# First modulation on TensorE with the condition stationary in four column groups, and the first norm's squares summed by TensorE

## The chip, the cores and the metric

One core of one Trainium2 chip runs the program; the other cores are idle. The metric is the time of one execution on the device, in microseconds, and the figure compared is the median of several executions.

The engines are named as in the profile: PE is TensorE (matmul), PEld its weight loads, DVE is VectorE, ACT is ScalarE, POOL is GpSimd, and SP is the queue that issues the DMAs here. Each engine takes its instructions in the order in which they stand in its own list and waits for semaphores; nothing overtakes within a list.

## The reference, cut to what matters

A block of a diffusion model with two layers. 512 latent tokens and 256 context tokens, 768 in all, have 1024 features. In each layer a condition vector, one for the latents and one for the context, is turned into six modulation vectors of 1024 values; the first two are the shift and the scale of the norm ahead of the input projection.

```
for i in range(DEPTH):                                    # DEPTH = 2
    mod_l = split(silu(c)     @ mod_w[i] + mod_b[i], 6)   # mod_w[i]: 1024 x 6144
    mod_c = split(silu(c_ctx) @ mod_w[i] + mod_b[i], 6)
    h_l = rms_norm(x,  g) * (1 + mod_l[1]) + mod_l[0]     # rms over the 1024 features
    h_c = rms_norm(xc, g) * (1 + mod_c[1]) + mod_c[0]
    p = h @ w_in[i]      # four mixers: rwkv7, differential attention, gla, grouped-query attention
    ...                  # mixers, w_out, second norm and modulation, convolutional feed-forward
```

All arithmetic that the kernel must match is float32. Nothing at all can be projected in layer 0 before the first two modulation vectors (16 blocks of 128 features, for two conditions) and the first norm's root are there.

## The kernel before

Activations lie with features on the 128 partitions: eight tiles of 128 features by 768 tokens, called x[0] to x[7]. A normed tile h[k] is kept as two numbers, a rounded high part and the rest, and so is each weight: ACT casts a staged weight (L377), POOL subtracts to get the rest (L378), and a product is three matmuls, high by high, high by rest and rest by high (`mm_feat`, L387; `mm_tok`, L710).

The part at issue is the head of the program, from the first instruction to the first matmul of the projection `glav` (L710) at 95.9 us. It is the generator `start()` in `run`, with `mod_first`, `squares` and `norm`:

- `mod_first` loads the condition twice. `cT` (128 x 16) is the condition with features on partitions. `silu_c` spreads each of the two condition vectors over all partitions (two tiles of 128 x 1024, each 512 KB of DMA) and applies silu to them with ACT (L432) and DVE (L433, L434).
- The eight x tiles are loaded (L1805); ACT squares each (L522), DVE adds the squares up over k (L526, six additions), and PE sums the two tiles that are left over the partitions (L552, 12 matmuls with one moving column). DVE takes the root by shifts and Newton steps (L400 to L407), spreads it along a diagonal (L563), and PE copies it to all partitions (L566); ACT brings it to SBUF (L570).
- Then a loop over k = 0 to 7. Pass k first makes the scale block and the shift block of its 128 features (`part(k)`), each by one of three ways, as the letters in `MOD0` say. P: PE, eight matmuls with a 128 x 128 weight block stationary and the two conditions moving (L465). D: DVE, one multiply with running sum per condition (L470, 128 x 1024). G: POOL multiplies (L474) and ACT sums (L475). Weights come in 16 loads of 512 KB (L461) into ten buffers. Then DVE scales x[k] into one shared tile y (L581), ACT writes the high part of h[k] (L583), and the rest comes from DVE (L585), or for k = 1, 4 and 7 from ACT and POOL (L588, L590). There is one y for all passes: the next pass's L581 waits until the last reader of y is done.
- PE meanwhile runs two projections that need h, `glaq` and `glak` (L387), 12 matmuls for each k as h[k] appears. When h[7] is done the mixers start; their first matmuls are those of `glav` (L710), six blocks of 128 tokens, each 24 matmuls over all eight k.

A scheduler takes the program in the order in which the code makes it, with `weave` mixing the generators of the mixers by due times, and decides in which order each engine gets its instructions. So an edit in the head can also move instructions of later parts.

## Time and profile before

| | us |
|---|---|
| three runs: median | 2406.66 |
| lowest, highest | 2404.67, 2407.81 |
| profiled execution, its time | 2409.76 |
| profiled execution, span from first to last instruction | 2408.0 |

| engine | busy us of the span | share | instructions |
|---|---|---|---|
| PE | 2209.1 | 92% | 15292 |
| DVE | 1457.9 | 61% | 3144 |
| POOL | 1040.0 | 43% | 1001 |
| ACT | 938.8 | 39% | 1756 |

The profiled execution is 3.1 us over the median. In the page's 40 slices PE is busy nine tenths almost everywhere; the first slice (60 us) has four tenths. The granted clock over the span is 0.945 of 2.4 GHz. In the column of the granted clock 1.00 stands also before the first record of a change, which is at 72.5 us here; ahead of that the clock is to be read from the length of the matmuls.

### The profile page before, as it was taken

The numbers are of one execution on the slowest core, as the hardware profiler recorded it, in microseconds if no ns is written. First come the engines' busy times: TensorE is split into PE (matmuls) and PEld (weight loads), VectorE is DVE, ScalarE is ACT, GpSimd is POOL, SyncE is SP. The second block draws the span as 40 slices with busy tenths as digits, with TensorE's granted clock in tenths as the row PEclk, the third lists the DMA queues.
The fourth block names the chain that finished last, engine by engine and source line by source line (L and its number), as shares of the span: only waits on it lengthen the run. The fifth ranks groups of instructions, "written<-read, shape, count | busy, mean of one in ns | idle before, by whom it ended". The sixth has DMA issues, their size and how long they took to land.

```text
span 2408.0 us, 40175 instructions
## 1 busy us (share of the span) xinstructions
PE 2209.1 (92%) x15292; PEld 1880.6 (78%) x15292; DVE 1457.9 (61%) x3144; ACT 938.8 (39%) x1756; POOL 1040.0 (43%) x1001
## 2 busy tenths in 40 slices
PE   4889988789988999999999989998899889999999
PEld 3777877577867888888888878777778668888888
DVE  6855689877774388655544662469777865322323
ACT  3333131355556242323222343322266474433333
POOL 3453465322331244434343645356433313655556
PEclk9889988688989999999999999998899899999999
DMA  6422264433225243333433432135433142233334
GB/s 246 146 90 73 78 186 123 106 87 84 65 65 167 66 136 118 114 105 108 137 100 111 152 102 62 58 92 153 116 86 94 47 123 84 89 104 89 104 92 136
DMA packets 232145, 258.48 MB, mean 107 GB/s; under 512 B 90960, under 2 KB 174224, under 8 KB 231952
## 3 DMA queue, kind: packets, MB, share of 16 engines
q1 hardware_dynamic: 231952, 255.92, 35.5%
q8 instruction: 120, 1.97, 0.3%
q14 instruction: 73, 0.60, 0.1%
HBM read 209.69 MB, written 37.77 MB: 103 GB/s over the span
## 4 chain that ended last, share of the span: by engine, by line
PE 63%; DVE 6%; POOL 4%; ACT 3%; issue 3%; DMA 2%; SPq 0%; POOLq 0%; DVEq 0%; ACTq 0%
PE pst L387 44%; PE pst L1552 5%; PE pst L427 4%; PE pst L710 3%; PE pst L977 2%; PE pst L1670 1%; PE pst L1675 1%; PE pst L941 1%; DVE mx L947 1%; ACT slab L949 1%; PE pst L944 1%; POOL slab L378 1%; DMA of<-slab 1%; POOL slab L846 0%; PE pst L1207 0%
## 5 line engine op out<-in xcount | busy, mean ns | idle before, releaser
L387 PE MATMUL pst<-slab,slab 128*128 128x512 f32 (+1 forms) x6552 | 1244.1, 351 | 20.5 <-ACT slab L583 7.4
L387 PEld LDWEIGHTS pst<-slab,slab 128*128 128x128 f32 x6552 | 1056.2, 191 | 201.5 <-ACT slab L583 10.8
L378 POOL TENSOR_TENSOR slab<-slab,slab 128x512 fp32r<-128x512 f32 (+1 forms) x428 | 576.8, 1357 | 724.1 <-ACT slab L377 701.9
L377 ACT CAST slab<-slab 128x512 fp32r<-128x512 f32 (+1 forms) x428 | 259.2, 614 | 575.4 <-PE pst L387 414.1
L710 PE MATMUL pst<-slab,slab 128*128 128x256 f32 (+1 forms) x1872 | 260.4, 300 | 11.0 <-POOL slab L378 11.0
L710 PEld LDWEIGHTS pst<-slab,slab 128*128 128x128 f32 x1872 | 249.1, 204 | 20.1 <-POOL slab L378 12.4
L623 DVE SCALAR_TENSOR_TENSOR slab<-pst,pp,slab 128x511 f32<-128x511 f32 x66 | 41.6, 658 | 305.1 <-ACT slab L620 305.1
L427 PE MATMUL pst<-cst,slab 128*128 128x128 f32 (+1 forms) x968 | 168.5, 309 | 51.2 <-POOL slab L1155 13.3
L497 DVE SCALAR_TENSOR_TENSOR slab<-slab,slab 128x512 bf16<-128x512 f32 x208 | 194.6, 936 | 6.1 <-DMA slab<-in_modw_dram 2.9
L427 PEld LDWEIGHTS pst<-cst,slab 128*128 128x128 f32 (+1 forms) x968 | 123.0, 155 | 79.5 <-POOL slab L1155 14.6
L1552 PE MATMUL pst<-slab,slab 128*128 128x128 f32 (+4 forms) x1328 | 167.3, 291 | 12.8 <-DVE slab L1606 4.0
L1552 PEld LDWEIGHTS pst<-slab,slab 128*128 128x128 f32 (+3 forms) x1328 | 139.6, 186 | 35.3 <-issue 10.5
L654 DVE SCALAR_TENSOR_TENSOR slab<-pst,fgate,slab 128x512 f32<-128x512 f32 (+1 forms) x144 | 88.0, 628 | 103.2 <-PE pst L387 103.1
L947 DVE TENSOR_REDUCE mx<-pst 128x1 f32<-128x768 f32 (+1 forms) x120 | 99.8, 846 | 33.5 <-PE pst L941 19.5
L949 ACT ACTIVATE slab<-pst,mx 128x768 f32<-128x768 f32 (+1 forms) x120 | 97.8, 816 | 46.5 <-DVE mx L947 43.0
L635 POOL TENSOR_TENSOR slab<-slab,slab 128x768 fp32r<-128x768 f32 (+1 forms) x44 | 74.0, 1683 | 63.9 <-ACT slab L634 63.9
L960 ACT ACTIVATE slab<-slab,r 128x768 f32<-128x768 f32 (+1 forms) x80 | 67.5, 852 | 9.3 <-DVE r L959 9.0
L977 PE MATMUL pst<-slab,slab 128*64 128x128 f32 x832 | 64.5, 287 | 2.8 <-DVE slab L424 1.5
L634 ACT CAST slab<-slab 128x768 fp32r<-128x768 f32 (+1 forms) x44 | 32.2, 732 | 84.1 <-DVE slab L631 84.0
L1639 POOL TENSOR_TENSOR slab<-cst,pcu 64x256 f32<-64x256 f32 x48 | 32.3, 673 | 72.7 <-PE pst L1552 18.5
L1425 DVE TENSOR_TENSOR slab<-slab,slab 96x31 f32<-96x31 f32 (+15 forms) x124 | 57.0, 459 | 8.7 <-DMA slab<-scrin 7.1
L629 ACT ACTIVATE slab<-slab 128x768 f32<-128x768 f32 (+1 forms) x44 | 32.5, 739 | 73.4 <-DVE slab L625 73.4
(309 smaller groups left out, 2707.7 us busy)
## 6 DMA issues: line engine op xcount, KB each, us to landing
slab<-in_wup_dram SPq DMA_DIRECT2D x88, 512.0 KB, 3.6
slab<-in_modw_dram SPq DMA_DIRECT2D x160, 256.0 KB, 3.0
slab<-in_wdn_dram SPq DMA_DIRECT2D x48, 512.0 KB, 3.5
slab<-in_win_dram SPq DMA_DIRECT2D x46, 512.0 KB, 3.7
slab<-in_modw_dram SPq DMA_DIRECT2D x16, 512.0 KB, 7.3
slab<-in_wout_dram SPq DMA_DIRECT2D x16, 512.0 KB, 3.5
slab<-in_xT_dram SPq DMA_DIRECT2D x16, 384.0 KB, 5.9
kb<-slab SPq DMA_DIRECT2D x8, 768.0 KB, 4.3
```

Of the source, the lines that this page charges most:

```text
L377: nc.scalar.copy(out=w[0], in_=st[:, k:k + q])
L378: nc.gpsimd.tensor_tensor(out=w[1], in0=st[:, k:k + q], in1=w[0].bitcast(F32), op=ALU.subtract)
L387: self.nc.tensor.matmul(ps[:, a:b], w[i][k][:, cols], x[j][k][:, a:b], start=(k == 0 and q == 0), stop=(k == nk - 1 and q == 2))
L427: self.nc.tensor.transpose(out, a.bitcast(F32) if a.dtype != F32 else a, self.c["ident"])
L497: self.tc.keep_in_program_order(nc.vector.scalar_tensor_tensor(out=junk, in0=w, scalar=1.0, in1=self.sc[s][:, e * hd:(e + 1) * hd], op0=AL ...
L635: nc.gpsimd.tensor_tensor(out=HL[:, 1, :n], in0=th[:, :n], in1=HL[:, 0, :n].bitcast(F32), op=ALU.subtract)
L654: nc.vector.scalar_tensor_tensor(out=x[m][:, a:b], in0=ps[:, a:b], scalar=gate[:, m, s:s + 1], in1=x[m][:, a:b], op0=ALU.mult, op1=ALU.add)
L710: self.nc.tensor.matmul(ps[:, :n], h[i][k][:, t * P:(t + 1) * P], w[j][k], start=(k == 0 and q == 0), stop=(k == KD - 1 and q == 2))
L947: nc.vector.tensor_reduce(out=mx, in_=sv, axis=AX.XY, op=ALU.max, negate=True)
L949: nc.scalar.activation(out=p[m][:, a:].rearrange("p (e c) -> p e c", e=2 - a // hb), in_=sv, func=AF.Exp, bias=mx, accum_out=lsum[:, m:m + 1])
L977: nc.tensor.matmul(acc[64 * e:64 * e + 64, :P], vs[e][:, i + j], aT[:, 256 * j + P * e:256 * j + P * e + P], start=(first and j == 0), sto ...
L1552: mm = lambda o, a, b, pos: nc.tensor.matmul(o, a, b, start=True, stop=True, tile_position=pos)
```

## The change

- Layout on the host: the 16 weight blocks of the first two modulation vectors are packed as eight pairs. Pair i holds blocks i (shift) and 8 + i (scale), 1024 input features by 256 output columns. Each pair is loaded in two halves of 512 KB into a ring of three pairs.
- `mod_open`: silu is applied to `cT` alone, and the two conditions are written into a zeroed tile c32 of 128 x 8 x 32, so that for each of the eight feature groups there is a stationary matrix of 32 columns, two of them not zero.
- `mod_pair`: for each pair eight matmuls, c32 stationary (32 columns), the weights moving (256 columns, float32). Feature group k goes to column group k mod 4 of the array, so that four partial sums stand on partitions 0, 32, 64 and 96 of one PSUM bank. ACT copies the 128 x 256 result to SBUF, and two matmuls with that copy stationary and a 128 x 2 selector (`sel`) moving add the four partial sums and turn features onto partitions. DVE adds the bias for both blocks at once (L473).
- The first norm's squares: ACT squares each x tile as before; PE sums each over partitions and over k in PSUM, 6 matmuls per tile, 48 in all (L1832), in place of the six DVE additions and 12 matmuls. `norm` takes the finished sum. Three buffers for squares are used in turn.
- `silu_c`, which makes the spread conditions that the later modulation parts need on DVE, is split into halves of 512 columns and moves out of the head, to the point where the mixers of layer 0 begin.
- In the head DVE, POOL and ACT no longer compute modulation blocks (L470, L474, L475 are gone).

```diff
-MOD0 = [(8 * (1 - _i % 2) + _i // 2, _e) for _i, _e in enumerate("PDGDPDGPDGDPDGDP")]
+MODP = [(_i, 8 + _i) for _i in range(8)]
...
+    c["sel"] = (i[:, None] % 32 == np.arange(2)[None, :]).astype(np.float32)
...
+    def mod_open(self):
+        nc = self.nc
+        c, th = self.small([P, KD, 2], "cT", 1), self.small([P, KD, 2], "cTt", 1)
+        nc.sync.dma_start(out=c, in_=self.A["cT"].rearrange("p (k s) -> p k s", s=2))
+        self.c32 = self.new([KD, 32])
+        nc.gpsimd.memset(self.c32, 0.0)
+        nc.scalar.activation(out=th, in_=c, func=AF.Tanh, scale=0.5)
+        nc.vector.scalar_tensor_tensor(out=c, in0=th, scalar=1.0, in1=c, op0=ALU.add, op1=ALU.mult)
+        nc.vector.tensor_scalar(out=self.c32[:, :, 0:2], in0=c, scalar1=0.5, scalar2=None, op0=ALU.mult)
+
+    def mod_pair(self, i, w, ps):
+        nc = self.nc
+        for k in range(KD):
+            g = 32 * (k % 4)
+            nc.tensor.matmul(ps[g:g + 32, 0:256], self.c32[:, k], w[k], start=(k < 4), stop=(k >= 4), tile_position=(0, g))
+        y = self.new([256])
+        nc.scalar.copy(out=y, in_=ps[:, 0:256])
+        for j in range(2):
+            nc.tensor.matmul(ps[:, 256 + 2 * j:258 + 2 * j], y[:, j * P:(j + 1) * P], self.c["sel"], start=True, stop=True)
+        a, b = MODP[i]
+        mb = self.par(0, "modb", a, b - a + 1)[:, ::b - a]
+        nc.vector.tensor_tensor(out=self.mod[0][:, a:b + 1:b - a], in0=ps[:, 256:260].rearrange("p (j s) -> p j s", s=2),
+                                in1=mb.unsqueeze(2).to_broadcast([P, 2, 2]), op=ALU.add)
...
     def mod_first(self):
-        self.silu(c, th)
-        self.silu_c()
-        ws, junk, jp = [self.new([D]) for _ in range(10)], self.new([D], BF16), self.new([D])
...
+        ws = [[self.new([4, 256]) for _ in range(2)] for _ in range(3)]
+        def load(m):
+            for q in range(2):
+                self.nc.sync.dma_start(out=ws[m % 3][q], in_=self.A["modp"][m][:, 4 * q:4 * q + 4])
+        for m in range(3):
+            load(m)
+        pss = []
+        for b in (2, 3):
+            pss.append((yield from self.bank(1, b, b + 1)))
+        def part(m):
+            w = [ws[m % 3][k // 4][:, k % 4] for k in range(KD)]
+            self.mod_pair(m, w, pss[m % 2])
+            if m + 3 < KD:
+                load(m + 3)
+            yield 100
...
         def start():
-            x, st = [self.new([T]) for _ in range(KD)], {}
-            first = yield from self.mod_first()
+            x, sq = [self.new([T]) for _ in range(KD)], [self.new([T]) for _ in range(3)]
+            ps = yield from self.bank(1, 4, 5)
+            self.mod_open()
             for k in range(KD):
                 nc.sync.dma_start(out=x[k], in_=xd[0][:, k])
-                self.squares(x, k, 0, T, st)
+                v = sq[k % 3]
+                nc.scalar.activation(out=v, in_=x[k], func=AF.Square)
+                for t in range(NT):
+                    nc.tensor.matmul(ps[:, t:t + 1], v[:, t * P:(t + 1) * P], self.c["ones"][:, 0:1],
+                                     start=(k == t == 0), stop=(k == KD - 1 and t == NT - 1))
+            st = {"sum": ps}
+            first = yield from self.mod_first()
...
             if li == 0:
+                self.silu_c()
                 streams.append(self.mod_part(0, range(16, 40), 8000))
```

In the lists of the engines the change shows at three places. Names such as slab_12_107 are pieces of SBUF; lines of the changed kernel are those of its own file (L388, L378, L379, L605, L610, L732 there are L387, L377, L378, L583, L588, L710 before).

The first place is ACT's list at passes 0 and 1 of the loop. In the kernel before, the weights of `glaq` and `glak` are cast among the squares (x is slab_10 and slab_11, squares go to slab_27), ahead of the loop:

```order
L522 ACTIVATE slab_27_135<-slab_10_105 128x768 x2
L522 ACTIVATE slab_27_135<-slab_11_106 128x768
L377 CAST slab_1_96<-slab_6_101 128x512 x2
L522 ACTIVATE slab_27_135<-slab_11_106 128x768
L377 CAST slab_2_97<-slab_7_102 128x512
L377 CAST slab_3_98<-slab_7_102 128x512
L570 COPY slab_33_197<-pst 128x768
```

In the changed kernel (y is slab_12_107, the h tiles of passes 0 and 1 are slab_27 and slab_28, L468 is the copy of a pair's partial sums):

```order
L468 COPY slab_5_100<-pst 128x256
L592 COPY slab_12_107<-pst 128x768
L605 ACTIVATE slab_27_240<-slab_12_107,mod_77 128x512
L605 ACTIVATE slab_27_240<-slab_12_107,mod_77 128x256
L468 COPY slab_6_101<-pst 128x256
L605 ACTIVATE slab_28_262<-slab_12_107,mod_77 128x512
L605 ACTIVATE slab_28_262<-slab_12_107,mod_77 128x256
L610 ACTIVATE slab_12_107<-slab_12_107,mod_77 128x512
L378 CAST slab_1_96<-slab_6_101 128x512 x2
L610 ACTIVATE slab_12_107<-slab_12_107,mod_77 128x256
L378 CAST slab_2_97<-slab_7_102 128x512
```

The casts have moved from ahead of the loop into pass 1, between the two halves of L610.

The second place is PE's list at the same two passes. Before (slab_34 is h[0], L387 a projection's matmul, L465 a block of the modulation):

```order
L566 MATMUL pst<-slab_33_197,cst 128x512
L566 MATMUL pst<-slab_33_197,cst 128x256
L465 MATMUL pst<-cT_107,slab_20_127 128x2 x8
L387 MATMUL pst<-slab_34_218,slab_1_96 128x512
L387 MATMUL pst<-slab_34_218,slab_2_97 128x512
```

In the changed kernel, from the first matmuls of h[1] (slab_28; slab_27 is h[0], slab_16 the first half of pair 3) on:

```order
L388 MATMUL pst<-slab_28_262,slab_1_96 128x512
L388 MATMUL pst<-slab_28_262,slab_1_96 128x256
L388 MATMUL pst<-slab_27_240,slab_2_97 128x512
L388 MATMUL pst<-slab_27_240,slab_2_97 128x256
L388 MATMUL pst<-slab_28_262,slab_1_96 128x512
L388 MATMUL pst<-slab_28_262,slab_1_96 128x256
L388 MATMUL pst<-slab_28_262,slab_1_96 128x512
L470 MATMUL pst<-cst,slab_6_101 128x2 x2
L466 MATMUL pst<-slab_16_180,slab_5_100 32x256 x4
L388 MATMUL pst<-slab_28_262,slab_1_96 128x256
```

The two matmuls that finish a pair (L470) now stand behind matmuls of the pass before, among them those that read the rest of h[1], which POOL writes.

The third place is ACT's list at the end of the loop, where the weights of `glav` are cast (the casts of 288 columns). Before, two thirds of them stand between the passes 5 to 7 (h tiles slab_39, slab_40 and slab_41):

```order
L583 ACTIVATE slab_39_324<-slab_33_197,mod_77 128x256
L377 CAST slab_3_98<-slab_5_100 128x288
L583 ACTIVATE slab_40_342<-slab_33_197,mod_77 128x512
L583 ACTIVATE slab_40_342<-slab_33_197,mod_77 128x256
L377 CAST slab_4_99<-slab_5_100 128x288 x2
L377 CAST slab_1_96<-slab_6_101 128x288 x2
L377 CAST slab_2_97<-slab_7_102 128x288
L583 ACTIVATE slab_41_364<-slab_33_197,mod_77 128x512
```

In the changed kernel (L749 and L748 bring the sums of `glak` and `glaq` to SBUF, L433 is the tanh of the spread conditions, in halves):

```order
L749 COPY slab_8_103<-pst 128x768
L433 ACTIVATE slab_7_102<-slab_6_101 128x512
L433 ACTIVATE slab_7_102<-slab_5_100 128x512
L433 ACTIVATE slab_19_183<-slab_19_183 128x512
L748 ACTIVATE slab_19_183<-pst 128x768
L433 ACTIVATE slab_18_182<-slab_7_102 128x512
L378 CAST slab_3_98<-slab_5_100 128x288
L378 CAST slab_4_99<-slab_5_100 128x288 x2
```

All eight casts now stand behind the evacuation of `glak` and `glaq` and the four tanh.

## Rows read from the trace of the kernel before

**Rows 1.** windows of 20 us: busy by engine, PEclk, DMA share, GB/s

```profile
20.00:40.00 20.00, 14.06 (x58) 12.77 (x58) 12.27 (x27) 6.14 (x10) 10.35 (x7) 1.00 0.86 338
...
60.00:80.00 20.00, 16.98 (x69) 14.47 (x69) 20.00 (x37) 8.31 (x16) 8.33 (x3) 0.90 0.37 141
80.00:100.00 20.00, 15.48 (x67) 12.86 (x67) 19.26 (x40) 8.49 (x19) 10.42 (x9) 0.67 0.46 160
100.00:120.00 20.00, 19.41 (x149) 19.20 (x149) 10.03 (x25) 5.79 (x12) 7.85 (x6) 1.00 0.42 134
```

**Rows 2.** PE groups by shape, 0 to 96 us: busy, mean ns, idle

```profile
L387 PE MATMUL pst<-slab,slab 128*128 128x512 f32 x48 | 27.7, 632 | 14.3 <-ACT slab L583 5.9 <-DVE slab L585 4.8 <-POOL slab L590 3.7
L387 PE MATMUL pst<-slab,slab 128*128 128x256 f32 x48 | 16.6, 399 | 0.0
L465 PE MATMUL pst<-cT,slab 128*128 128x2 f32 x80 | 15.7, 327 | 0.2 <-DVE mod L466 0.2
L552 PE MATMUL pst<-cst,slab 128*128 128x1 f32 x24 | 5.3, 353 | 22.7 <-DVE slab L526 22.7
```

**Rows 3.** DVE group, 38 to 96 us: busy us, mean ns, idle

```profile
L470 DVE SCALAR_TENSOR_TENSOR slab<-slab,slab 128x1024 bf16<-128x1024 f32 x12 | 17.2, 1430 | 0.0
```

**Rows 4.** timeline 0 to 140 us, up to the loop: start us, us, instruction

```profile
5.30 0.22 ACT L432 ACTIVATE cTt<-cT 128x16 f32<-128x16 f32 x1 [3.31 <-DMA cT<-in_cT_dram]
...
8.71 1.06 ACT L432 ACTIVATE slab<-slab 128x1024 f32<-128x1024 f32 x1 [3.19 <-DMA slab<-in_cr_dram]
...
10.08 1.77 ACT L522 ACTIVATE slab<-slab 128x768 f32<-128x768 f32 x2 [0.31 <-DMA slab<-in_xT_dram]
...
22.73 5.28 PE L552 MATMUL pst<-cst,slab 128*128 128x1 f32 x24 [22.73 <-DVE slab L526]
...
28.25 1.57 DVE L400 TENSOR_SCALAR t<-ms 128x6 int32<-128x6 int32 x1
...
30.06 2.19 DVE L405 TENSOR_TENSOR t<-r 128x6 f32<-128x6 f32 x1
...
34.64 2.93 PE L566 MATMUL pst<-slab,cst 128*128 128x512 f32 x4 [3.21 <-DVE slab L563]
...
37.60 0.80 ACT L570 COPY slab<-pst 128x768 f32<-128x768 f32 x1 [13.02 <-PE pst L566]
...
38.44 0.75 DVE L581 SCALAR_TENSOR_TENSOR slab<-slab,gs,slab 128x512 f32<-128x512 f32 x1 [1.11 <-ACT slab L570]
```

**Rows 5.** timeline 55 to 120 us, the loop and its end: same columns

```profile
68.59 4.32 PE L387 MATMUL pst<-slab,slab 128*128 128x512 f32 x12 [1.42 <-ACT slab L583]
...
78.28 1.14 DVE L581 SCALAR_TENSOR_TENSOR slab<-slab,gs,slab 128x512 f32<-128x512 f32 x2
79.05 1.12 ACT L583 ACTIVATE slab<-slab,mod 128x512 fp32r<-128x512 f32 x2 [4.43 <-DVE slab L581]
...
84.54 5.63 POOL L378 TENSOR_TENSOR slab<-slab,slab 128x288 fp32r<-128x288 f32 x5 [3.16 <-ACT slab L377]
...
91.14 1.98 POOL L590 TENSOR_TENSOR slab<-slab,slab 128x768 fp32r<-128x768 f32 x1 [0.98 <-ACT slab L588]
...
93.17 2.93 PE L387 MATMUL pst<-slab,slab 128*128 128x512 f32 x8 [2.28 <-POOL slab L590]
...
95.90 21.76 PE L710 MATMUL pst<-slab,slab 128*128 128x288 f32 x163
...
99.49 0.37 ACT L731 COPY slab<-pst 128x256 f32<-128x256 f32 x1 [2.21 <-PE pst L710]
```

**Rows 6.** timeline of PE, 168 to 186 us: matmuls in row and column groups

```profile
172.46 1.62 PE L1170 MATMUL pst<-slab,slab 64*32 64x64 f32 x96
174.01 4.16 PE L387 MATMUL pst<-slab,slab 128*128 128x512 f32 x20
```

**Rows 7.** window over that burst, L1170 alone: PE, PEld, clock, DMA

```profile
172.40:174.00 1.60, 1.54 (x96) 1.38 (x96) 0.50 0.00 0
```

**Rows 8.** window of 50 us in layer 0's mixers: as rows 1

```profile
350.00:400.00 50.00, 42.04 (x295) 37.87 (x294) 47.25 (x97) 12.88 (x26) 32.79 (x25) 0.83 0.42 125
```

More of the change, by code (lines that the diff above doesn't have):

```diff
@@ L133, in pack @@
     mw = g["mod_w"].transpose(0, 2, 1).reshape(L * 48, P, D)
-    A["modw0"] = np.stack([mw[m].reshape(P, KD, P).transpose(2, 1, 0).reshape(P, D) if e == "P" else mw[m] for m, e in MOD0])
+    A["modp"] = np.stack([np.concatenate([mw[m].reshape(P, KD, P).transpose(2, 1, 0) for m in q], axis=2) for q in MODP])
     A["modw"] = mw[16:]
@@ L438, in silu_c @@
         self.sc = []
+        hd = D // 2
         for s in range(2):
[L440 to L476 removed]
@@ new lines, in silu_c @@
+            self.sc.append([])
+            for e in range(2):
+                v, th = self.new([hd]), self.new([hd])
+                self.nc.sync.dma_start(out=v, in_=self.A["cr"][s:s + 1, e * hd:(e + 1) * hd].to_broadcast([P, hd]))
+                self.silu(v, th)
+                self.free(th)
+                self.sc[s].append(v)
+    def mod_open(self):
[7 more added lines that the diff above has]
+        nc.vector.tensor_scalar(out=self.c32[:, :, 0:2], in0=c, scalar1=0.5, scalar2=None, op0=ALU.mult)
@@ L477, in part @@
             yield 100
-            if k == KD - 1:
-                self.free(*ws, junk, jp, ps)
+            if m == KD - 1:
+                self.free(*sum(ws, []), *pss, self.c32)
         return part
@@ L1784, in ffn_mod @@
         yield from self.mod_part(1, range(48), 9500)
-        self.free(*self.sc)
+        self.free(*self.sc[0], *self.sc[1])
     def run(self):
```

49 lines of the change are left out of this document (12 added, 37 removed).

## The prediction

> **What bounds the kernel now.** I read the windows first, then the groups by engine in the first 96 us, then the timeline there. The change touches the head alone, so a gain is what the head's end (95.90 us, the first `glav` matmul) comes forward, as far as later parts keep it. In the loop DVE is full: 20.00 and 19.26 of 20 us, while PE has 16.98 and 15.48 [rows 1]. Of DVE's time 17.2 us are L470, the blocks of the modulation, at 1430 ns each [rows 3]. From the first L581 (38.44) to the last `glak` matmul (93.17 + 2.93 = 96.10) the eight passes take 57.7 us [rows 4, 5]. PE's own work in the head is heavy all the same: 44.3 us of L387, 15.7 of L465, 5.3 of L552 [rows 2]. Most of it runs at 1.2 GHz: 12 matmuls of one pass, 4608 columns, take 4.32 us, where `glav` at the full clock takes 21.76 / 163 = 0.1335 us for 288 columns [rows 5], which would be 2.14 us for a pass. So with DVE relieved PE and its clock are the next bound.
>
> **The squares.** Before: PE begins at 22.73, when DVE has added up, and ends at 28.01 [rows 4]. After: 48 matmuls are 96 passes of 5.28 / 24 = 0.22 us, 21.1 us in all; that exceeds the loads and ACT's 0.88 us per tile, so PE bounds it. These matmuls have one moving column, and the rows show the same kind at 0.22 us without a rise, so I keep that level. They begin when the first x has landed and is squared. cT is there at 5.30, and the first square runs at 10.08 behind a 512 KB load of the condition that leaves the head [rows 4]. I take 6.6 + 0.88 = 7.5 (ends 6.2 and 11.0). The sum is done at 28.6 (27.3 to 32.1). Six DVE additions vanish, and nothing is won by that.
>
> **Root and spread.** From 28.01 to the first L566 it takes 6.63 us. Two DVE rows in it take 1.57 and 2.19 us, for instructions of some 0.2, while POOL multiplies [rows 4]; POOL is idle there after the change, so 3.4 us go. L588 then starts at 28.6 + 3.2 = 31.8, takes 2.93, and the copy 0.80 [rows 4]. Pair 0's matmuls fit ahead of it. With two short DVE instructions the first L603 starts at 36.0 instead of 38.44.
>
> **A pair.** A float32 pass costs 2.93 / 1536 = 1.9 ns a column at half the clock [rows 4], 0.49 us for 256 columns. A pair has 16 passes: 7.8 us one after the other. 96 passes of 64 columns in row and column groups took 1.62 us at a granted 0.50 [rows 6, 7], 17 ns each instead of 122: over eight places of the array they overlap seven times. Four column groups should overlap nearly four times, 2.0 us a pair at half and 1.0 at the full clock (ends 2.0 and 7.8). The Trainium skill (TensorE: Matmul & The Clock Gate, Measured speedup vs the span model) gives 2.38 for three column groups; by that a pair would take 3.3 us at half the clock, and no row here has column groups alone. The two matmuls that finish a pair are four passes like L552's, 0.9 us (0.45).
>
> **Passes 0 and 1.** The copy of pair 1 stands in ACT behind pass 0's L605, so pass 1 begins 4.0 us after pass 0: 0.75 + 1.12 + 0.37 + 0.9 and short waits [rows 4, 5]. Pass 2 is later still. L470 of pair 2 stands in PE behind matmuls that read the rest of h[1]. That rest is POOL's (L612, 1.98), which waits for two splits of 1.3, and these for a cast that now stands in ACT behind half of L610 [rows 5]. Summed: 1.14 for L603, 1.1 for the rest of L605 and half of L610, 0.6 for a cast, 2.6, 2.0, 1.1 for three matmuls, 0.9, and 1.2 for short instructions: 10.6 us. Pass 2 begins at 36.0 + 4.0 + 10.6 = 50.6.
>
> **Passes 2 to 7.** PE has 4.32 + 0.9 + 2.0 = 7.2 us of work a pass at half the clock and 3.6 at the full one. The chain of one pass (L603 1.14, half of L605, the copy 0.37, L470, short DVE steps and latencies) is some 4.2, more at k = 4, where POOL is in it. So 4.2 and 7.2 are the ends. Where PE was busy 15.5 to 17 of 20 us the granted clock was 0.67 and 0.90 [rows 1]; this will be alike, so 4.8 us, and the last pass begins at 74.6. Its tail: L603 1.14, 0.5 of L605, 1.12 of L610, 1.98 on POOL, eight matmuls 1.9: 81.2 instead of 96.10. The Trainium skill (TensorE: Matmul & The Clock Gate, HAM oscillation) warns that matmul bursts with waits between them run each burst cold. By that rule, the trace agrees (0.67 at 80 to 100 us): every pass would cost 7.2.
>
> **What gives most of it back.** The loads of `glav`'s weights are issued after the last pair frees c32, and the casts stand in ACT behind the copies of `glak` and `glaq` and four tanh that left the head's start: 0.8 + 4 x 0.53 (half of 1.06) + 0.8 + 0.4 = 4.2 us [rows 4, 5]. Then POOL splits eight pieces at 5.63 / 5 = 1.13 us, 9.0 us [rows 5]. Before, casts and splits were covered by the loop; that cover is gone. So `glav`'s first block of tokens is complete at 81.2 + 4.2 + 9.0 = 94.4, and its other 120 matmuls take 16.0, with 1.5 more for a start at half the clock: 111.9. Before it was 95.90 + 144 x 0.1335 = 115.1. **3.2 us are left of 14.9.** The moved silu also costs DVE and ACT some 4 us each in the mixers, where neither is full at that time.
>
> **Later parts.** The scheduler reorders layer 0's mixers: 144 of the projection matmuls stand earlier in PE's list, and one direction of the rwkv blocks (L1396) stands among the other's recursion (L1552) rather than ahead of it. There DVE is the fuller engine, 47.25 of 50 us against PE's 42.04 [rows 8], and its work is the same. I take 0, with 10 us either way, about the 8 us that PE idles in that one window.
>
> **Sum.** Against the profiled execution: 2409.76 - 3.2 = 2406.6. The median stands 3.1 below it: 2403.5. A measurement of this kernel can tell about 0.2%, 4.8 us, from no change.
>
> **Rivals.**
> - *The full clock holds.* Denser matmuls keep 2.4 GHz, a pass costs 4.2 and `glav` starts warm: 3.0 + 1.5 more, 2399. For it: 1.00 from 100 us on, when PE never waits [rows 1]. Against it: in the loop it will wait.
> - *PE at half the clock bounds the loop (slower).* It decides where a pass costs more than some 5.4 us; at 7.2 it adds 5 x 2.4 = 12.0, and the head ends later than before: 2415.5. For it: the loop before, mostly at 1.2 GHz. Against it: rises came as soon as PE was full.
> - *Column groups don't overlap* (the change would not do what it says). A pass then has 13.0 us of PE work at half and 6.5 at full; at some 8.8, with 6 more in passes 0 and 1, 2429. Rows 6 and 7 speak against it.
> - *Layer 0's new order* wins or loses 10 us: 2393.5 or 2413.5. The move of matmuls speaks for an effect, the full DVE against a large one.
>
> **How the numbers follow.** Forecast 0.40 (0.31 of it within 0.2%, 0.09 faster), its own range 2399 to 2408; full clock 0.20; half the clock 0.13; no overlap 0.04; order better 0.12, worse 0.11. Faster 0.41, same 0.31, slower 0.28. The range 2391 to 2417 leaves out the third rival and about half of the tails of the fourth and second.
>
> **What would show it.** Squares on PE without a gap from about 7.5 to 28.6 us; first L603 near 36; a gap before pass 2; passes of 4 to 6 us after it, with the clock going up and down; the loop's last matmul near 81; then a PE gap until casts at about 85 and a slow first block of `glav`. If pairs take over 4 us the overlap is wrong; if `glav`'s second block starts before 90, the give-back is; if the head's gain is there and the time isn't, look for it between 300 and 500 us.

## The result and the profile after

The changed kernel takes 2432.3 us (median of four runs, 2427.32 to 2447.93), the kernel before on the same chip 2407.23 (2404.67 to 2411.70): a ratio of 1.011, 95% interval 1.0082 to 1.0139, so **slower by about 1%**, where 2403.5 in a range of 2391 to 2417 was forecast. The profiled execution of the changed kernel takes 2429.32 us, 19.6 more than that of the kernel before.

I read the head first. The timeline of the changed kernel, the rows that answer to [rows 4, 5] (L603 is the old L581, L588 the old L566, L388 the old L387; L466 are the pairs):

```profile
8.90 20.64 PE L1832 MATMUL pst<-cst,slab 128*128 128x1 f32 x96 [8.90 <-ACT slab L1830]
29.47 1.93 PE L466 MATMUL pst<-slab,slab 128*32 128x256 f32 x16
32.74 2.93 PE L588 MATMUL pst<-slab,cst 128*128 128x512 f32 x4 [1.34 <-DVE slab L585]
...
36.88 1.15 DVE L603 SCALAR_TENSOR_TENSOR slab<-slab,gs,slab 128x512 f32<-128x512 f32 x2
...
49.83 0.16 DVE L473 TENSOR_TENSOR mod<-pst,pp 128x4 f32<-128x4 f32 x1 [8.49 <-PE pst L470]
...
50.28 1.15 DVE L603 SCALAR_TENSOR_TENSOR slab<-slab,gs,slab 128x512 f32<-128x512 f32 x2
...
72.81 1.15 DVE L603 SCALAR_TENSOR_TENSOR slab<-slab,gs,slab 128x512 f32<-128x512 f32 x2
...
77.66 2.04 PE L388 MATMUL pst<-slab,slab 128*128 128x512 f32 x8 [2.33 <-POOL slab L612]
```

The squares run without a gap to 29.5, the first pass starts at 36.9, there is the long gap before pass 2 (8.49 us of DVE idle), and the loop's last matmul ends at 77.66 + 2.04 = 79.7 where it ended at 96.1. So the loop has come 16.4 us forward.

Then the start of `glav`, the same view, and below it the one row of the waits of SP's queue (76 to 92 us: what waited, for what, us in total, times, longest):

```profile
79.75 0.80 ACT L749 COPY slab<-pst 128x768 f32<-128x768 f32 x1 [3.92 <-PE pst L388]
...
83.21 0.33 SPq L445 DMA_DIRECT2D slab<-in_cr_dram  x1
83.58 1.39 SPq L372 DMA_DIRECT2D slab<-in_win_dram  x3
...
88.03 0.63 ACT L433 ACTIVATE slab<-slab 128x512 f32<-128x512 f32 x1 [3.40 <-DMA slab<-in_cr_dram]
89.28 2.86 ACT L378 CAST slab<-slab 128x288 fp32r<-128x288 f32 x8 [0.61 <-DMA slab<-in_win_dram]
...
89.78 11.07 POOL L379 TENSOR_TENSOR slab<-slab,slab 128x288 fp32r<-128x288 f32 x9 [12.17 <-ACT slab L378]
...
100.04 0.37 ACT L753 COPY slab<-pst 128x256 f32<-128x256 f32 x1 [2.68 <-PE pst L732]
...
117.17 0.37 ACT L753 COPY slab<-pst 128x256 f32<-128x256 f32 x1
```

```profile
SPq L445 <- DVE slab L434: 9.3, 1, 9.3
```

`glav`'s weight loads (L372) are issued only at 83.6, because the fourth load of the condition (L445) stands ahead of them in SP's queue and waits 9.3 us for a buffer that DVE's silu (L434) still reads. Casts at 89.3, then POOL's splits at 1.23 us each, first block done at 100.4 (99.9 before, [rows 5]). The sixth block's copy, at 117.17, comes 1.7 us after that of the kernel before, whose row is

```profile
115.43 0.37 ACT L731 COPY slab<-pst 128x256 f32<-128x256 f32 x1
```

So all of the 16.4 us are given back before 118 us, and 1.7 us more; the other 18 of the 19.6 us are lost later. The windows show the hole (columns as in [rows 1]):

```profile
60.00:80.00 20.00, 17.26 (x121) 11.44 (x119) 10.39 (x23) 7.85 (x17) 3.63 (x2) 0.97 0.70 242
80.00:84.00 4.00, 0.00 (x0) 0.00 (x0) 2.62 (x5) 2.40 (x5) 0.00 (x0) 0.50 0.01 2
84.00:88.00 4.00, 0.00 (x0) 0.00 (x0) 1.07 (x4) 0.63 (x1) 0.00 (x0) 0.50 0.74 212
...
96.00:100.00 4.00, 3.65 (x12) 2.61 (x12) 3.62 (x9) 0.62 (x1) 4.00 (x4) 0.50 0.77 252
100.00:120.00 20.00, 19.41 (x141) 19.21 (x139) 9.89 (x24) 5.15 (x11) 5.67 (x5) 0.93 0.37 118
```

The granted clock fell from 1.00 to 0.50 just before that hole: 0.97 over 60 to 80 us puts the fall 1.2 us before 80, in the loop's last eight matmuls and behind their 2.33 us of waiting. It stayed at 0.50 through the hole and up to 100 us, so `glav`'s first block ran at half the clock.

**Where the time went.** Three matmuls mark the program further on: the spreads of the root in the second norm of layer 0, in the first norm of layer 1 and in its second norm. The timeline of PE at those places, changed kernel first, then the kernel before:

```profile
850.47 2.93 PE L588 MATMUL pst<-slab,cst 128*128 128x512 f32 x4 [2.50 <-DVE slab L585]
...
1424.94 2.93 PE L588 MATMUL pst<-slab,cst 128*128 128x512 f32 x4 [2.49 <-DVE slab L585]
...
2057.95 0.75 PE L588 MATMUL pst<-slab,cst 128*128 128x256 f32 x2 [2.77 <-DVE slab L585]
```

```profile
838.53 2.93 PE L566 MATMUL pst<-slab,cst 128*128 128x512 f32 x4 [2.49 <-DVE slab L563]
...
1414.51 2.93 PE L566 MATMUL pst<-slab,cst 128*128 128x512 f32 x4 [2.49 <-DVE slab L563]
...
2037.95 0.70 PE L566 MATMUL pst<-slab,cst 128*128 128x256 f32 x2 [2.77 <-DVE slab L563]
```

The lag is 1.7 us at 117, 11.9 at 850, 10.4 at 1425 and 20.0 at 2058. So **layer 0's mixers lose 10 us and layer 1's mixers, 1300 us after the last edited instruction, lose another 10**. The feed-forward part between loses nothing; by the traces the lists of PE and DVE are the same there in both kernels, while in layer 0's mixers about a third of PE's and half of DVE's instructions stand elsewhere in the list, and in layer 1's about a ninth and a third.

The same stretches as windows, from the sixth `glav` copy to the spread and between the two norms of layer 1, changed kernel first, then the kernel before:

```profile
117.54:850.47 732.93, 632.32 (x5255) 530.34 (x5254) 485.51 (x1224) 295.03 (x606) 271.09 (x324) 0.90 0.34 99
1424.94:2057.95 633.01, 562.45 (x4711) 475.79 (x4711) 395.95 (x917) 279.86 (x555) 258.78 (x309) 0.92 0.31 88
```

```profile
115.80:838.53 722.73, 641.29 (x5255) 539.27 (x5253) 497.71 (x1224) 294.31 (x605) 274.34 (x324) 0.90 0.35 100
1414.51:2037.95 623.44, 559.01 (x4710) 473.41 (x4711) 399.31 (x917) 280.03 (x555) 256.39 (x309) 0.93 0.32 90
```

PE stands idle for 100.6 us in layer 0 instead of 81.4, and for 70.6 in layer 1 instead of 64.4 (the stretch less PE's busy time).

In layer 0 the loss can be seen at work. Windows of 50 us of the changed kernel, then the second of the two of the kernel before (its first is [rows 8]):

```profile
350.00:400.00 50.00, 46.06 (x356) 42.52 (x354) 42.81 (x118) 13.03 (x25) 18.31 (x16) 1.00 0.36 111
400.00:450.00 50.00, 18.22 (x107) 13.97 (x110) 33.96 (x79) 9.15 (x21) 30.06 (x45) 0.50 0.30 78
```

```profile
400.00:450.00 50.00, 39.76 (x291) 34.82 (x290) 41.60 (x129) 10.47 (x30) 21.15 (x36) 0.67 0.51 127
```

From 400 to 450 PE is busy for 18.2 us instead of 39.8, at a granted 0.50 instead of 0.67. The timeline says why. L1378 (the old L1356) is the scan that opens the feature step of one direction and block of rwkv; the third and fourth scans are the second direction's. Changed kernel (DVE and PE), then the kernel before (DVE):

```profile
387.29 1.74 DVE L1378 TENSOR_TENSOR_SCAN slab<-reset,slab 128x768 f32<-128x768 bf16 x1
...
391.30 3.13 PE L732 MATMUL pst<-slab,slab 128*128 128x256 f32 x24
...
407.72 1.74 DVE L1378 TENSOR_TENSOR_SCAN slab<-reset,slab 128x768 f32<-128x768 bf16 x1
...
419.36 0.47 PE L428 MATMUL pst<-cst,slab 128*128 128x128 f32 x1 [22.38 <-POOL slab L1606]
```

```profile
348.91 1.76 DVE L1356 TENSOR_TENSOR_SCAN slab<-reset,slab 128x768 f32<-128x768 bf16 x1
...
375.75 1.75 DVE L1356 TENSOR_TENSOR_SCAN slab<-reset,slab 128x768 f32<-128x768 bf16 x1
```

The second direction's features come 32 to 38 us later, behind nearly all of the first direction's inverse on DVE. The projections (L732), which before lay between the second direction's matmuls until 418.7 us, are used up at 394.4, and PE then stands still for 22.4 us: the work that could have covered the wait had been moved ahead of it. In layer 1 no such wait stands out: the longest of PE is 9.0 us there, and 10.2 in the kernel before.

### The profile page after: what moved, and what is told of

The parts are those of the page before. It is cut to its first block, busy times and chain, and to the rows that moved or that the text cites. A ratio compares the mean times of both kernels' runs of the same rounds, so it can differ in the third digit from the quotient of the medians.

```text
span 2427.5 us, 40389 instructions
## 1 busy us (share of the span) xinstructions
PE 2215.3 (91%) x15444; PEld 1876.3 (77%) x15444; DVE 1407.0 (58%) x3106; ACT 933.9 (38%) x1750; POOL 1018.4 (42%) x994
## 4 chain that ended last, share of the span: by engine, by line
PE 66%; DVE 11%; POOL 5%; ACT 3%; issue 3%; DMA 2%; SPq 0%; POOLq 0%; DVEq 0%; ACTq 0%
PE pst L388 44%; PE pst L1574 5%; PE pst L428 4%; PE pst L732 3%; PE pst L999 2%; PE pst L1692 2%; PE pst L1697 1%; DVE slab L1447 1%; POOL slab L379 1%; DVE slab L1449 1%; PE pst L963 1%; DVE mx L969 1%; ACT slab L971 1%; DVE slab L516 1%; PE pst L966 1%
## 5 line engine op out<-in xcount | busy, mean ns | idle before, releaser
L388 PE MATMUL pst<-slab,slab 128*128 128x512 f32 (+1 forms) x6552 | 1235.6, 350 | 12.6 <-POOL slab L612 5.1
L388 PEld LDWEIGHTS pst<-slab,slab 128*128 128x128 f32 x6552 | 1048.4, 190 | 195.5 <-POOL slab L612 9.6
L379 POOL TENSOR_TENSOR slab<-slab,slab 128x512 fp32r<-128x512 f32 (+1 forms) x428 | 574.3, 1351 | 747.5 <-ACT slab L378 721.6
L378 ACT CAST slab<-slab 128x512 fp32r<-128x512 f32 (+1 forms) x428 | 258.9, 612 | 579.6 <-PE pst L388 435.1
L732 PE MATMUL pst<-slab,slab 128*128 128x256 f32 (+1 forms) x1872 | 255.8, 297 | 20.2 <-ACT slab L378 10.1
L732 PEld LDWEIGHTS pst<-slab,slab 128*128 128x128 f32 x1872 | 243.8, 200 | 31.5 <-POOL slab L379 14.1
L428 PE MATMUL pst<-cst,slab 128*128 128x128 f32 (+1 forms) x968 | 169.9, 309 | 90.9 <-DVE slab L888 29.6
L516 DVE SCALAR_TENSOR_TENSOR slab<-slab,slab 128x512 bf16<-128x512 f32 x252 | 229.2, 909 | 6.6 <-DMA slab<-in_modw_dram 3.1
L1574 PE MATMUL pst<-slab,slab 128*128 128x128 f32 (+5 forms) x1304 | 167.1, 285 | 8.7 <-DVE slab L1669 2.7
L1574 PEld LDWEIGHTS pst<-slab,slab 128*128 128x128 f32 (+3 forms) x1304 | 137.7, 180 | 30.1 <-issue 10.6
L1661 POOL TENSOR_TENSOR slab<-cst,pcu 64x256 f32<-64x256 f32 x48 | 31.9, 665 | 96.1 <-PE pst L1574 23.5
L999 PEld LDWEIGHTS pst<-slab,slab 128*64 128x64 f32 x832 | 47.5, 143 | 16.5 <-issue 5.4
```

The source lines that it names most:

```text
L378: nc.scalar.copy(out=w[0], in_=st[:, k:k + q])
L379: nc.gpsimd.tensor_tensor(out=w[1], in0=st[:, k:k + q], in1=w[0].bitcast(F32), op=ALU.subtract)
L388: self.nc.tensor.matmul(ps[:, a:b], w[i][k][:, cols], x[j][k][:, a:b], start=(k == 0 and q == 0), stop=(k == nk - 1 and q == 2))
L428: self.nc.tensor.transpose(out, a.bitcast(F32) if a.dtype != F32 else a, self.c["ident"])
L516: self.tc.keep_in_program_order(nc.vector.scalar_tensor_tensor(out=junk, in0=w, scalar=1.0, in1=self.sc[s][e], op0=ALU.mult, op1=ALU.mult, ...
L732: self.nc.tensor.matmul(ps[:, :n], h[i][k][:, t * P:(t + 1) * P], w[j][k], start=(k == 0 and q == 0), stop=(k == KD - 1 and q == 2))
```

## The experiments

Every ratio is against the kernel before on the same chip, with its 95% interval; the kernel before ran from 2402 to 2421 us on the chips used, so plain times of different calls are not compared. "Places" means which SBUF buffers and PSUM banks the program's own allocator gives to a tile. It hands out what was released longest ago, so that an edit in the head changes what the mixers get, and with it which instruction must wait for whose last read; the scheduler then lists the instructions otherwise.

The table holds, for each profiled execution, the end of the loop, the end of the sixth `glav` block's copy, the time from there to the spread in layer 0's second norm ("layer 0"), and the time between the two norms of layer 1 ("layer 1"). All from timeline rows like those above.

| kernel | order of the mixers | ratio | loop end | `glav` 6 | layer 0 | layer 1 |
|---|---|---|---|---|---|---|
| before | before | 1 | 96.1 | 115.8 | 722.7 | 623.4 |
| changed | changed | 1.011 | 79.7 | 117.5 | 733.0 | 633.0 |
| e1 | before | 1.000 (0.9983 to 1.0018) | 90.9 | 118.0 | 730.4 | 619.3 |
| e2 | changed | 1.0049 (1.0030 to 1.0068) | 84.6 | 103.5 | 738.2 | 640.9 |
| e3 | changed | 1.009 (1.0067 to 1.0113) | 73.5 | 112.0 | 735.5 | 639.3 |
| e4 | before | 1.0015 (0.9999 to 1.0031) | 103.9 | 124.0 | 722.6 | 619.3 |
| e5 | before | 0.9997 (0.9980 to 1.0014) | 85.7 | 115.3 | 729.5 | 624.0 |
| e6 | before | 0.9967 (0.9951 to 0.9983) | 85.5 | 106.7 | 719.5 | 625.7 |
| e7 | another | 1.0025 (1.0011 to 1.0039) | 93.1 | 116.2 | 712.9 | 634.7 |
| e8 | another | 1.0076 (1.0050 to 1.0101) | 78.7 | 110.1 | 738.4 | 638.5 |
| e9 | before | 0.9977 (0.9963 to 0.9992) | 82.0 | 112.3 | 726.4 | 627.2 |
| e10 | before | 0.9934 (0.9917 to 0.9951) | 82.0 | 102.2 | 724.7 | 618.1 |
| e11 | another | 0.9936 (0.9919 to 0.9952) | 77.4 | 111.3 | 706.8 | 625.3 |
| e12 | another | 1.0046 (1.0030 to 1.0063) | 82.6 | 110.5 | 718.9 | 642.4 |
| e13 | e11's | 0.9913 (0.9895 to 0.9931) | 80.3 | 98.3 | 708.3 | 627.1 |
| e14 | another | 1.0018 (1.0006 to 1.0030) | 96.3 | 117.2 | 719.2 | 631.0 |
| e15 | e11's | 0.9902 (0.9875 to 0.9929) | 71.9 | 90.1 | 718.1 | 627.7 |
| e16 | e11's | 0.9897 (0.9878 to 0.9915) | 79.4 | 97.5 | 712.6 | 625.3 |

By the traces, the kernels that the table puts under one order have the same lists behind `glav` (line, operation and shape, engine by engine), but for a few instructions at their start. Executions of one order still differ: the seven of the old order lie between 719.5 and 730.4 in layer 0 and between 618.1 and 627.2 in layer 1, so single entries say little where they differ by less than that. PE's idle time differs less: 80.5 to 84.8 us in layer 0 for the seven and 99.4 to 100.6 for the three of the changed order, 62.6 to 64.4 against 68.6 to 71.0 in layer 1. What differs within an order is mostly how long the same matmuls took: in e1, the longest of the seven, PE was busy for 648.8 us at a granted 0.89, in e6, the shortest, for 639.0 at 0.90.

**One part alone: e3 and e4.** e3 has the new modulation and the old squares:

```diff
-                for t in range(NT):
-                    nc.tensor.matmul(ps[:, t:t + 1], v[:, t * P:(t + 1) * P], self.c["ones"][:, 0:1],
-                                     start=(k == t == 0), stop=(k == KD - 1 and t == NT - 1))
+                self.squares(x, k, 0, T, st)
```

> One part alone: the new modulation (pairs in four column groups, silu moved) with the squares added up on DVE as before. The mixers' order is that of the changed kernel. Theory A: the loss stays, 2428 to 2437, the head some 2 us later. Rival C (the 96 passes of one column on PE are what costs): 2405 to 2412.

e4 is the reverse: the kernel before, with the removed loop in place of the added line, and the modulation and the silu as they were.

> The other part alone: the squares summed by PE, the modulation and the silu as before. The mixers' order is that of the kernel before. Theory A: no loss, 2405 to 2411 (the x tiles land behind the condition's loads, so the sum is done at 30 to 33 instead of 28.0, and the root runs without waits). Rival C: 2425 or more.

e3 is 1.009, e4 1.0015. The loss sits in the modulation part of the change (with the silu that it moves), and it goes with the changed order, which e3 has and e4 has not; rival C, the one-column passes on PE, falls. Two guesses were wrong. e4's 2416 us is above the 2405 to 2411 expected, though its ratio isn't clear of 1. And e3's head is not 2 us later but 6 us earlier (loop end 73.5). While DVE adds the squares up, PE makes the first two pairs and finishes them ahead of the spread; in the changed kernel PE is held by the squares until 29.5 and has only the eight matmuls of pair 0 ahead of it. e4's `glav` is 8 us later than that of the kernel before: its squares begin at 11.3, behind the condition's loads, and end at 31.9 instead of 28.0, so that the spread is 3.2 us later, and the loop adds the rest, for a reason that isn't shown. By the ratio's interval between 0 and 7 us of it reach the end.

**The order given back: e1, e5 and e9.** In these the head computes as the changed kernel does, but allocates and releases in the sequence of the kernel before; its tiles lie in the old ten weight buffers.

```diff
-        ws = [[self.new([4, 256]) for _ in range(2)] for _ in range(3)]
+        ws = [[self.shaped(self.hw[2 * m + q], [4, 256]) for q in range(2)] for m in range(3)]
...
-        for b in (2, 3):
-            pss.append((yield from self.bank(1, b, b + 1)))
+        pss = [self.hps, self.pst[:, 2048:2560]]
...
+            self.hw, self.hjunk = [self.new([D]) for _ in range(10)], [self.new([D], BF16), self.new([D])]
```

With that alone every engine's list behind the head is that of the kernel before again. The three differ in the silu and the squares. e1 calls the silu in the last pass; e5 sends its loads in pass 4 and computes at the mixers' start; e9 is e5 with

```diff
-                v = self.new([T])
+                p, v = self.new([T]), self.hw[6 + k % 3][:, :T]
```

where `p` only keeps the sequence of allocations.

> The changed kernel, with its buffers in the head put where the kernel before has them (the same sequence of allocations and releases, the new tiles laid into the old ten weight buffers) and the four silu pieces issued in the code of the last pass. Every engine's list in layer 0's mixers is then again in the order of the kernel before. Theory A (the head is as forecast, the loss is the order that the mixers took when the head's buffers moved): 2404 to 2410 us, no PE wait of over 10 us between 395 and 435, the head's last loop matmul near 80. Rival B (the order is innocent; the loss comes from the new head, its clock, or the silu done later): 2425 to 2435 as the changed kernel.

> As e1 (the buffers of the head where the kernel before has them), but the four loads of the condition go out after the last weight load and the silu itself is computed at the start of the mixers, so that DVE's four silu pieces no longer stand ahead of the last pass. Theory A: the last glak matmul back at about 80 (84 to 88 in e1), glav's first block ends near 96 to 98, the sixth near 113; the mixers as before. Against the kernel before on the same chip a ratio of 0.997 to 1.000. Rival D (what the head wins is given back in the mixers in any case, since DVE bounds them): 1.000 to 1.002, the projections' end earlier and the recursion's start not.

> As e5, with the squares in three buffers in turn as the changed kernel has them: in e1, e5 and e6 the squares from the fourth on shared one buffer, ACT and PE took turns, and the root came 6 us later (first L566-type matmul at 38.5 to 38.8 instead of 32.7). So this is the changed kernel's head with the mixers' order of the kernel before. Theory A: loop end at 80, sixth glav block at 109 to 111 (115.8 before), ratio 0.995 to 0.999. Rival B, in a weaker form (part of the loss belongs to the new head whatever the order): above 1.001. Rival D: glav early, the ratio at 0.999 to 1.001.

The loss is gone in all three: 1.000, 0.9997, 0.9977, against 1.011. Rival B (the new head, its clock, the late silu) falls. e1 says it most plainly: its sixth `glav` block ends at 118.0, as late as the changed kernel's 117.5, and still the whole loss is gone. e9 lies within the range expected of it, e5 at the upper end of its own and e1 just above, both with a later head than expected, and the reason is mine: in e1 and e5 (and e6) the squares from the fourth on share one buffer. The timeline of ACT in e6:

```profile
17.22 0.84 ACT L1869 ACTIVATE slab<-slab 128x768 f32<-128x768 f32 x1 [2.86 <-PE pst L1871]
20.92 0.84 ACT L1869 ACTIVATE slab<-slab 128x768 f32<-128x768 f32 x1 [2.86 <-PE pst L1871]
```

ACT waits for PE and PE for ACT, 3.7 us a tile instead of 2.6, and the root comes 6 us late. In e1 the silu stood ahead of the last pass besides (loop end 90.9). e9 has neither, and at the place where the changed kernel stands still its PE does this:

```profile
390.13 5.41 PE L738 MATMUL pst<-slab,slab 128*128 128x256 f32 x24
395.47 0.46 PE L1424 MATMUL pst<-slab,slab 64*64 64x64 f32 x16
395.86 3.13 PE L738 MATMUL pst<-slab,slab 128*128 128x256 f32 x24
398.92 0.46 PE L1424 MATMUL pst<-slab,slab 64*64 64x64 f32 x16
...
419.34 1.48 PE L428 MATMUL pst<-cst,slab 128*128 128x128 f32 x4 [2.69 <-POOL slab L1612]
```

A projection of 24 matmuls (L738) between every two blocks of the second direction (L1424), and a wait of 2.7 us where there was one of 22.4.

**Places moved under the old head: e7 and e14.** The kernel before, with its buffers released in reverse, and with one unused buffer held through the head:

```diff
-                self.free(*ws, junk, jp, ps)
+                self.free(ps, jp, junk, *ws[::-1])
```

```diff
+            pad = self.new([512])
             x, st = [self.new([T]) for _ in range(KD)], {}
             first = yield from self.mod_first()
+            self.free(pad)
```

> The kernel before with one line changed: the buffers of the head's modulation are released in the reverse order. The head is the same instruction by instruction; only which buffers the mixers of layer 0 get, and so their order, differs (about a fifth of DVE's and a tenth of PE's instructions stand elsewhere). Theory A: the order alone moves the time, so a ratio outside 0.998 to 1.002 is likely, either way, up to 1%. Rival B: 0.999 to 1.001.

> The kernel before with one unused buffer of 512 columns held through the head, so that the head's later buffers lie elsewhere; no instruction is added. A second other order of the mixers under the old head, beside e7. Theory A: outside 0.998 to 1.002 again, either way. If the order of the kernel before is a good one among those at hand: above 1.002.

1.0025 and 1.0018. No work was added or taken away, and both are measurably slower, though by far less than 1%. e14's mark of 0.998 to 1.002 was not left, so for the size of the effect these two say a quarter of a per cent. My text on e7 was not exact: the release also moved some instructions inside the head, and the loop ended at 93.1. What it shows best is in the table: layer 0 10 us faster and layer 1 11 us slower than the kernel before, from one line, and both outside what the seven executions of the old order span.

**Other orders under the new head: e8, e11 and e12.** The changed kernel with the silu called within the modulation stream (e11), with the silu in two tiles of 1024 columns in place of four of 512 (e8), and with the silu in pass 4 (e12):

```diff
             if li == 0:
-                self.silu_c()
                 streams.append(self.mod_part(0, range(16, 40), 8000))
...
     def mod_part(self, li, ms, dt):
+        if ms[0] == 16 and li == 0:
+            self.silu_c()
+            yield 1000
```

```diff
-        hd = D // 2
+        hd = D
```

```diff
                 load(m + 3)
+            if m == 4:
+                self.silu_c()
```

These are e11, e8 and e12 in turn.

> The changed kernel with silu_c in two pieces of 1024 columns in place of four of 512, at the same point. The head up to the last pass is the same; the buffers that the mixers get differ, and with them the order. Theory A: another time than the changed kernel's 1.011, by more than 0.003 either way, and no stall of 20 us of PE on POOL where the changed kernel has it, or one elsewhere. Rival B: 1.009 to 1.013 again.

> The changed kernel with silu_c called within the stream of the modulation parts, at the same point of the program give or take one yield. The head up to the last pass is the same; buffers and order of the mixers are a third kind, on PE nearer to the kernel before than the changed kernel is (some 1300 of 12500 instructions elsewhere, against 1800). Theory A: a time of its own, likely between 1.000 and 1.010, and the stretches that change against the changed kernel are layer 0's and layer 1's mixers. Rival B: 1.009 to 1.013 again.

> The changed kernel with silu_c, allocation and all, moved into pass 4 of the loop behind the last weight load. A fourth order of the mixers. Theory A: glav's first block 3 to 6 us earlier than in the changed kernel (the fourth condition load no longer stands ahead of glav's), the rest by its own order, between 1.000 and 1.012. Rival B: 1.007 to 1.011, the changed kernel less these 3 to 6 us.

1.0076, 0.9936, 1.0046. All four silu placements, the changed kernel's 1.011 included, compute the same and have their sixth `glav` block between 110 and 118; they spread over 1.7%, 42 us, of which their heads' 7 us are 0.3 points. e8 by itself isn't clear of the changed kernel (1.0050 to 1.0101 against 1.0082 to 1.0139); e11 and e12 are. e11 came out below everything expected of it. e8 ends `glav` 7 us ahead of the changed kernel and is still slower than the kernel before by 0.76%: its layer 0 takes 738.4.

One piece of my own theory doesn't hold. I took the late second direction for the price in layer 0, and it is late with a long wait of PE in the changed kernel, e2 and e3. But e12 has it as well (scans at 373.6 and 399.7) and needs only 718.9 for layer 0, while e11, the fastest there, has long waits of its own, for weights. The waits of PE from 110 to 840 us (us in total, times, longest), the first row of e12 and then the first of e11:

```profile
PE pst L428 <- POOL slab L1608: 20.3, 3, 19.8
```

```profile
PE pst L734 <- POOL slab L379: 19.5, 4, 11.5
```

So a single long wait, even of 20 us, is not what an order costs; what follows can take it back. That the order as a whole sets the time is shown; which of its waits do is not.

**Does the head's gain add to the order? e2, e6, e10, e13, e15, e16.** e2 is the changed kernel with `glav`'s weights ahead of the loop:

```diff
-            self.early.update({q: self.win(0, q, 0, KD) for q in ("glaq", "glak")})
+            self.early.update({q: self.win(0, q, 0, KD) for q in ("glaq", "glak", "glav")})
```

The ring of weights has no room for a third set, so that some of `glaq`'s and `glak`'s products here read `glav`'s weights; the instructions are the same in number and shape.

> The changed kernel, with the loads, casts and splits of glav's weights issued before the loop (as glaq's and glak's are); the mixers' order stays that of the changed kernel. Both theories: glav's first block ends near 90 instead of 100, its last copy near 108 instead of 117. Theory A: what is won reaches the projections' end (near 385 instead of 394) but the stall behind it waits for DVE and POOL, so only part of the 9 us is kept: 2422 to 2432. If the time falls by the full 9 us, to 2418 to 2421, the stall hangs on PE's pace and not on DVE and POOL. Rival B: no less than 2425.

1.0049: 14 us earlier at `glav`, and 0.6 points better than the changed kernel. The stall is as long as before (22.40 us) and stands 11.6 us earlier, so no more than 2.4 of the 14 us are lost up to there, fewer than expected; by the ratios all 14 may reach the end, each being uncertain by 0.2 to 0.3 points.

e6, e10 and e13 load `glav`'s weights behind the last pair, split the first three feature groups within the loop and the other five on DVE after it:

```diff
+        for k in range(3):
+            cast(k, nc.gpsimd)
...
+            for k in range(3, KD):
+                cast(k, nc.vector)
```

e6 is e5 with that, e10 is e9 with that, e13 is e11 with that, e16 is e13 once more; e15 is e13 with DVE's squares.

> As e5, and glav's three weight loads go out right after the last pair's; the first three feature groups are cast and split within the loop, the other five after it, split by DVE in place of POOL. Theory A: glav's first block ends near 88, its sixth near 106, 9 us before that of the kernel before; ratio 0.994 to 0.998. Rival D: the sixth block is early all the same, but the ratio stays at 0.999 to 1.002.

> As e6, with the squares in three buffers in turn. Theory A: sixth glav block at 101 (106.7 in e6, 115.8 before), ratio 0.992 to 0.996, that is 2 to 6 us better than e6. Rival D: no better than e6's 0.9967.

> e11 with glav's weights early as in e10 (three loads behind the last pair's, three feature groups split in the loop, five by DVE after it); the mixers' order is e11's. If the head and the order add up: sixth glav block at 101 to 102 (111.3 in e11), ratio 0.988 to 0.991, that is 6 to 9 us below e11. If the early glav is taken back by waits in e11's order: 0.9925 to 0.995.

> e13 with the squares added up by DVE as in the kernel before; the mixers' order is e13's. In e3, the changed kernel with DVE's squares, PE made the first three pairs while it waited for the root, and the loop ended at 73.5 instead of 79.7. If PE's 20.6 us of squares is what keeps the loop late: loop end near 74, sixth glav block near 93 (98.3 in e13), 4 to 6 us below e13. If the loop's end is set by the pair loads or the full clock anyway, no more than 2 us below e13.

> e13 once more, for a comparison with e15 on the same chip: 0.990 to 0.993 of the kernel before.

Under the old order `glav` earlier by 8.6 us (e5 to e6) and 10.1 us (e9 to e10) took 0.30 and 0.43 points off, 7 and 10 us: what the head wins there is kept, within the 5 us or so that such differences of ratios are uncertain by, and rival D (the mixers give it back in any case) falls for this range. Under e11's order 13.0 us (e11 to e13) took off 0.23 points, and by e16's reading 0.39: 5.5 to 9.4 us of 13 to 14; e13 itself fell between the two marks set for it. e15 ends the loop 7.5 us before e16 and `glav` 7.4, and comes out the same (0.9902 against 0.9897): layer 0 took 718.1 instead of 712.6. So the squares on PE do cost 6 to 7 us in the head; under this order no gain from that is seen at the end, though the two intervals would still allow some 6 us. **e13 beats both kernels**, 0.9913 and 0.9897 in its two measurements (e15 by as much), 1% below the kernel before and, going by the ratios, 2% below the changed one.

## Why the prediction was wrong, point by point

- *Squares, root and spread*: right. Done at 29.5 (28.6), first L603 at 36.9 (36.0). "Nothing is won by that" fell short: by e3 the squares hold PE while it could make pairs, and the loop ends 6 us later for them.
- *A pair*: right at half the clock, where 16 passes took 1.93 us (2.0); at the full one 8 took 0.64, so 1.3 a pair instead of 1.0. By 7.8 / 1.93 the four groups overlap four times. The Trainium skill (TensorE: Matmul & The Clock Gate, Measured speedup vs the span model) has 2.38 for three column groups, by which a pair was estimated at 3.3; the trace shows 1.93.
- *Passes and loop end*: right in size. 3.3 us to pass 1 (4.0), 10.1 to pass 2 (10.6), then 4.5 a pass (4.8); loop end 79.7 (81.2). But 4.8 was reckoned from a clock that goes up and down and a PE that waits, and in part from a misreading: the 0.90 for 60 to 80 us holds the 1.00 that stands ahead of the first record at 72.5, while a pass at 68.59 still took 4.32 us, its length at half the clock. In the changed kernel PE hardly waited in passes 2 to 7, busy for 24.7 of the 24.8 us from 50.2 to 75; pass 2 took 6.3 us (0.50 from 48 to 52 us, 0.64 from 52 to 56), and the five passes that begin from 56.6 to 72.8 lie 4.1 us apart (1.00 from 56 to 60, 0.97 from 60 to 80). That the mean came out near 4.8 is in part luck. The Trainium skill's warning of cold bursts with waits between them (TensorE: Matmul & The Clock Gate, HAM oscillation) was not put to the test in these passes. The clock fell behind a wait of 2.33 us ahead of the loop's last matmuls, and there the trace agrees.
- *What gives most of it back*: the mechanism was right, the term mis-sized. Forecast 4.2 (its terms add up to 4.1) + 9.0 from the loop's end to `glav`'s first block, measured 100.4 - 79.7 = 20.7. The prediction counted the moved silu's four tanh in ACT, and not its four loads in SP's queue: the fourth waits for a buffer of the first silus, and `glav`'s loads stand behind it. The prediction named the move of a step and left out one of the queues that it is moved into. 3.2 us left became 1.7 lost.
- *Later parts, 0 with 10 us either way*: **this step failed**, and it is most of the miss: of the 22.8 us by which the profiled executions miss the forecast, the term above has 4.9 and this one 17.9. The mean of the changed order's three executions (changed, e2, e3) against the seven of the old order is 735.6 to 725.1 us in layer 0 and 637.7 to 622.4 in layer 1: 10.5 and 15.3 us. The 10 us were taken from PE's idle time in one window of layer 0, which bounds what a better order can win there and not what a worse one can lose; and layer 1, which the edit doesn't touch, was not counted, though its order had moved as well. The move itself, 144 projection matmuls ahead of the second direction, could have been a warning, since filler is then spent before the wait that it covers; I read it as a gain or a loss alike. That it is the price isn't shown: e12 spends its projections ahead of that direction too and needs 718.9.
- *The rivals*: "layer 0's new order worse" was the right one, with a chance of 0.11; its 10 us are what layer 0 lost, and layer 1 lost as much or more again. The full clock held in the second half of the loop, as the first rival had it, but `glav` did not start warm, and the gain went with the rest.

e12 bears out what the fourth load cost: its four loads go out in pass 4, and its loads for `glav` are issued at 74.6 instead of 83.6,

```profile
74.63 1.58 SPq L372 DMA_DIRECT2D slab<-in_win_dram  x3
```

so that its first `glav` block is done at 94.1, 11.5 us behind its loop's end at 82.6, where the changed kernel takes 20.7 and 13.2 was forecast.

With both put right, the old order given back and the silu's loads sent in pass 4 (e9), the forecast is met: 2403.5 against 2406.66 was 0.9987, and e9 measures 0.9977 (0.9963 to 0.9992).

What stays open: whether an order costs by the lists themselves or by the waits for reused buffers that made the scheduler choose them. In all of these kernels both move together. Open too are what makes up the loss in layer 1 and which waits decide.

## What to carry to other kernels

Where an allocator and a scheduler set the order of what follows, an edit has two effects, its own and a new order of everything behind it; here the two together came to between -0.6% and +1.1% for one and the same computation, while the heads differed by 0.3 points. Measure an edit with the order held (the same sequence of allocations, as in e9) before judging it, and try a few orders afterwards, since one line that moves buffers may be worth more than the edit. And when a step is moved, follow its loads into the DMA queue as carefully as its arithmetic into the engines: what stood behind a 9.3 us wait there was the next stage's weights.

## What the runs showed of the hardware

- PE was busy for 20.6 us on end with the squares (one moving column a pass, 0.215 us each), and the matmuls behind them still ran at half the clock: the 16 passes of the first pair took 1.93 us, 0.97 for eight. Eight passes of a pair took 1.08 us where the granted clock was 0.50 (48 to 52 us), and 0.64 where it was 1.00 (56 to 60 us):

```profile
49.66 1.08 PE L466 MATMUL pst<-slab,slab 128*32 128x256 f32 x8
...
56.14 0.64 PE L466 MATMUL pst<-slab,slab 128*32 128x256 f32 x8
```

- Float32 matmuls in four column groups of 32, all with the same 128 rows, overlapped four times at half the clock (7.8 / 1.93, above).
